# Seven edits in one kernel: sums through 2 KB rows, a merge order that lags one branch, chunked groups, quadrant matmuls, paired retention heads, norms moved behind other work, and a last tile in halves

## The chip, the cores and the metric

The kernel runs on one core of a Trainium2 chip. The metric is the device time of one execution, in microseconds (us); lower is better. Three executions of the kernel before took 3305.34 us in the median (3305.04 to 3309.78).

## The reference, cut to what matters

Two stacks of two layers each run over one sequence of 512 tokens with 1024 channels, all in float32.

```python
for l in range(2):                       # first_block
    h = rmsnorm(x, norm1_g[l]); p = h @ w_in[l]
    y_rw  = rwkv7_branch(...)            # 8 heads of 64, a state recurrence over 512 steps, group norm
    y_ret = retention_branch(...)        # 4 heads, scores * decay @ v, norm per head
    y_sg  = sgu_branch(...)              # 4 groups, spatial gating
    x = x + sum(sigmoid(gates) * (branch @ w_branch[l])) @ w_out[l]
    x = x + conv_ffn(rmsnorm(x, norm2_g[l]), ...)
x = rmsnorm(x, final_g)
for l in range(2):                       # second_block: five attention branches, same kind of merge
    x = _layer(x, mem, ...)
return rmsnorm(x, final_norm)
```

## The kernel before, in words

Activations lie channels by tokens: eight tiles of 128 channels x 512 tokens. Every weight is split into a rounded high part and a low rest (`whi`, `wlo`, by ScalarE at L159 and VectorE at L160), and every product is three matmuls (`mm3`, L168 to L170: high x high, high x low, low x high). A weight chunk is 128 x 1024 (512 KB); one chunk serves one output tile of 24 matmuls of 512 columns (`fm_tile`, `fm_steps`). Two chunks are in flight at most (two buffers each of raw, high and low).

In a layer of the first stack a planner (`Plan`) writes out the order of TensorE's instructions by hand. It knows dense steps (projections, cost 1.4 for six matmuls) and chain steps, which carry a cost and a wait after which the next step of that chain is due; dense steps fill the waits. Ranks: the projections of the rwkv branch first, then retention and gating unit (`branches`), then the 24 gate tiles (`gates1`). The chains are: `rw_pair` for each of four pairs of heads f, then `rwkv_inverse`, then two lanes of `rw_unit` (16 units per layer, each with the chain pst, psam, psv, psg, psh, psu, psy and psx), then `rw_final` per pair. A unit of pair f > 1 waits until `rw_final` of pair f - 2 has ended.

`sums` adds over the channels of a head: a matmul with a selector puts the sums of the four token groups on rows 32 g + i, a function makes the tile `sums` of them, a DMA writes this 128 x 128 tile to memory, and n DMAs (n is 2 for pairs, 1 for retention) read it back spread over all partitions, in pieces of 128 tokens (512 bytes). After a sum the chain waits 13 (L519), 10 (L737) or 11 (L750) units of the plan, and retention's `ret_end` 12.

`retention` takes one head after the other. Per head and token block j it makes scores with a contraction of 64 rows (`pssc`, L804; head e lies on rows 64 e to 64 e + 63), multiplies them with the decay (`pret`, L807), and accumulates `psret` (L809). `tm_group` projects token-major tiles: for each of four token groups it runs through both chunks of the contraction, 24 matmuls of 256 columns.

`merge` (after the plan; here the framework orders TensorE) goes through eight output tiles c and in each through the branches n, in the order retention, gating unit, rwkv. `pbr` is the branch product; each tile of the first stack holds 12 matmuls. Two PSUM banks serve `pm` and `pbr` in the first stack. `split` of the rwkv result is at L181 and L182.

`end_norm` and `end_norms` (between the stacks two norms in one) sum squares with tiny matmuls (`psn`), take root and reciprocal (`rcol`), and spread the result with matmuls (`psb`). At the start the splits of x, its squares and their sums are made tile by tile. At the end the last `w_out` tile is followed by `end_norm`, eight multiplications (L1816) and eight DMAs to the output.

Of the kernel before, what the change touches and what calls it, by code (L numbers as in the profile page):

```python
# [18 lines left out]
S = 512  # L19
D = 1024  # L20
# [86 lines left out]
class Kern:  # L107
# [7 lines left out]
    def __init__(self, tc, I, out, dbg=None, cfg=None):  # L115
        self.tc, self.nc, self.I, self.out = tc, tc.nc, I, out
        self.dbg_outs = dbg or {}
        self.cfg = cfg or {}
# [77 lines left out]
    def sums(self, x, sel, n, ps, out, fn):  # L196

        nc = self.nc
        for g in range(4):
            nc.tensor.matmul(ps[32 * g:32 * g + 32, :], lhsT=sel, rhs=x[:, g * 128:(g + 1) * 128],  # L200
                             start=True, stop=True, skip_group_check=True)
        t = self.ap.tile([128, 128], F32, name="sums", tag="sums", bufs=2)
        fn(t, ps)
        d = self.dp.tile([4, 32, 128], F32, name="sumd", tag="sumd", bufs=8)
        nc.sync.dma_start(d.rearrange("g r t -> (g r) t"), t)
        for i in range(n):
            nc.sync.dma_start(out[i * 128 // n:(i + 1) * 128 // n, :].rearrange("p (g t) -> p g t", g=4),
                              d[:, i][None].to_broadcast([128 // n, 4, 128]))
# [161 lines left out]
    def fm_steps(self, ws):  # L370

        ps = self.PM(name="pm")
# [6 lines left out]
    def tm_group(self, src, evac):  # L379

        ws = [self.weights(src[i], 1024) for i in range(2)]
        for g in range(4):
            ps = self.PM([128, 512])
            for k in range(KD):
                w = ws[k // 4]
                o = (k % 4) * 256
                hh = (self.h[k][0][:, g * 128:(g + 1) * 128], self.h[k][1][:, g * 128:(g + 1) * 128])
                self.mm3(ps[:, :256], hh, (w[0][:, o:o + 256], w[1][:, o:o + 256]), k == 0, k == KD - 1)
                if k == KD // 2 - 1:
                    yield MORE  # L390
            evac(g, ps[:, :256])
            yield MORE if g < 3 else TILE
# [73 lines left out]
    def rw_pair(self, l, f, r, k, vt, m, lora, half):  # L466
# [52 lines left out]
        yield Chain(0.4, 13.0)  # L519
# [89 lines left out]
    def rw_unit(self, f, g, st, lane):  # L609
# [79 lines left out]

        for c in range(2):  # L690
            psx = self.P([128, 2, 64], "psx")
            cs = slice(64 * c, 64 * c + 64)
            for e in range(2):
                os = ws = slice(64 - 64 * e, 128 - 64 * e)
                us = slice(64 * e, 64 * e + 64)
                b_ = tk[cs, 0, us]
                nc.tensor.matmul(psx[os, 0, :], lhsT=uw[cs, e, ws], rhs=b_, start=True, stop=True,
                                 skip_group_check=True)
                nc.tensor.matmul(psx[os, 1, :], lhsT=b_, rhs=uw[cs, e, us], start=True, stop=False,
                                 skip_group_check=True)  # L700
                nc.tensor.matmul(psx[os, 1, :], lhsT=tk[cs, 1, us], rhs=vp[cs, 3 * e, :], start=False, stop=True,
                                 skip_group_check=True)
            nc.vector.tensor_tensor(xt[:, 2 * g + c, :], psx[:, 0], self.ident64, op=OP.add)
            nc.scalar.activation(cc[:, 2 * g + c, :], psx[:, 1], AF.Copy)
        yield Chain(2.4, 0.5)

    def rw_final(self, l, f, st):
# [29 lines left out]
        yield Chain(0.4, 10.0)  # L737
# [12 lines left out]
        yield Chain(1.6, 11.0)  # L750
# [15 lines left out]
    def retention(self, l, win):  # L766
# [4 lines left out]
        for f in range(2):  # L771
# [18 lines left out]
            ws = self.stream([win[l, 22 + 2 * f], win[l, 23 + 2 * f]])  # L790
            for e in range(2):
                h = 2 * f + e
# [4 lines left out]
                dec = F(name="dec"); nc.sync.dma_start(dec, I["c_dec1"][h])  # L797
                yield Chain(0.0, 1.0)
                hs = slice(64 * e, 64 * e + 64)
                psy = self.PF(name="psret")  # L800
                for j in range(4):
                    n = S - 128 * j
                    ps = self.PF(name="pssc")
                    nc.tensor.matmul(ps[:, :n], lhsT=qk[1][hs, j * 128:(j + 1) * 128], rhs=qk[0][hs, j * 128:],  # L804
                                     start=True, stop=True)
                    p = T(name="pret")
                    nc.vector.tensor_tensor(p[:, :n], ps[:, :n], dec[:, :n], op=OP.mult)  # L807
                    yield Chain(0.3 + n / 1024, 3.2)
                    nc.tensor.matmul(psy[:, j * 128:], lhsT=vt[j // 2][:, j % 2, e * 128:(e + 1) * 128], rhs=p[:, :n],  # L809
                                     start=(j == 0), stop=(j == 3), skip_group_check=True)  # L810
                y = self.tile("Y", name="yret")
                sq = T(name="sqr")
                nc.scalar.activation(sq, psy, AF.Square)
                nc.vector.scalar_tensor_tensor(y, psy, 0.5, gt, op0=OP.mult, op1=OP.mult)
                yield Chain(0.4, 3.0)
                self.norms(sq, self.sel[:, 1], 1, self.PF([128, 128], "psrn"), bias=self.eps[:, 0:1], scale=1.0 / 128)
                self.plan.add(self.ret_end(l, h, y, sq), 0, 12.0)
                yield Dense(0.4)
# [104 lines left out]
    def merge(self, l, ys, wbr, wout, gain, stag=None, split=True):  # L923
        nc = self.nc
        nb = len(ys)
        s, late = [], []
        ws = self.stream(wbr[l])
        for c in range(KD):
            acc = None
            for n in range(nb):  # L930
                if (c, n) in self.gd:
                    g = self.F(name="gate")
                    nc.sync.dma_start(g, self.gd[c, n])
                else:
                    g = self.gate(self.gs, "F")
                nc.scalar.activation(g, g, AF.Tanh, scale=0.5)  # L936
                pb = self.fm_tile(ws, ys[n], name="pbr")
                with self.tc.high_priority(offset=self.cfg.get("hp", self.AHEAD)):
                    nc.vector.scalar_tensor_tensor(g, g, 1.0, pb, op0=OP.add, op1=OP.mult)  # L939
                if late and n == self.cfg.get("ln", 1):  # L940
                    s.append(self.split(late.pop(), *stag(c - 1), scale=0.5))
                if acc is not None:
                    (nc.gpsimd if self.pre and n in self.cfg.get("pa", (1, 2, 3)) else nc.vector).tensor_tensor(g, g, acc, op=OP.add)  # L943
                acc = g
            self.dump("%ss%d_%d" % (self.pre, l, c), acc)
            late.append(acc)
        s.append(self.split(late.pop(), *stag(c), scale=0.5))
# [3 lines left out]
        for c in range(KD):  # L951
# [8 lines left out]
            self.norm_step(c, x, gain(c) if gain else None, split=split)  # L960


    def ffn(self, l, next_gain, gain1, side):
# [32 lines left out]
        if gain1:  # L996
            self.end_norms()
        else:
# [204 lines left out]
    def block2_layer(self, l, gain):  # L1203
# [6 lines left out]
        self.zd = []  # L1210
        fill = self.gates(I["w_gt2"][l][10:], 5, self.cfg.get("e2", (5, 4, 4, 5, 4, 3, 4, 5)))
# [83 lines left out]
        self.end_norm(copy=gain is not None)  # L1295

    def col(self, name, scale=None, tag="F"):
        return self.evac2(self.fm_tile(self.ws), name, scale, tag)
# [461 lines left out]
    def run(self):  # L1760
# [3 lines left out]
        with ExitStack() as ctx:  # L1764
# [11 lines left out]
            if L1:  # L1776
                g12 = self.cp.tile([128, 8], F32, name="g12")
                nc.vector.tensor_tensor(g12, V[:, 16:24], V[:, 24:32], op=OP.mult)
                with block(self, "act"):
                    self.begin_norm()  # L1780
                    self.first = self.stream(I["w_in1"][0, 0:14])
# [309 lines left out]
```

## Time and profile before

| what | us |
|---|---|
| median of three executions | 3305.34 |
| the profiled execution | 3305.33 |
| its span in the profile | 3303.6 |
| TensorE busy (matmuls) | 3231.0 |
| VectorE busy | 2188.8 |
| ScalarE busy | 1365.9 |

The span is cut in windows and rows of time; a row of a timeline has its start, its length, the engine, the line, the operation, what is written and read, shapes and a count, and in brackets the idle time before it with what ended it. TensorE's matmuls are pipelined, so the length of a row overlaps the next; the time that a matmul takes is read from start to start. A matmul in plain float32 shows as two records. The granted clock 1.00 is 2.4 GHz, 0.50 is 1.2 GHz.

### The profile page before, as it was taken

The page shows a single profiled execution, that of the slowest core. Times are in us where ns is not written, and L with a number is a line of the kernel's source. Part 1 is how long each engine was busy: PE and PEld are TensorE (multiplying, and loading weights), DVE is VectorE, ACT ScalarE, POOL GpSimd, SP SyncE. Part 2 cuts the span into 40 slices and gives each one's busy share as a digit, 9 for nine tenths or more (in the row PEclk, how much of TensorE's full clock was granted, in tenths as well). Part 3 has the DMA queues.
Part 4 walks back from the last instruction along what each step waited for, and adds up shares of the span by engine and source line. Part 5 has one row for each costly group of instructions (what it writes and reads, how often), then busy time and mean ns, then how long its engine had stood idle before and what let it go on. Part 6 is the DMA issues. An engine that isn't in the chain of part 4 may idle for free.

```text
span 3303.6 us, 47422 instructions
## 1 busy us (share of the span) xinstructions
PE 3231.0 (98%) x17956; PEld 2594.5 (79%) x17960; DVE 2188.8 (66%) x4062; ACT 1365.9 (41%) x2440; POOL 125.6 (4%) x176
## 2 busy tenths in 40 slices
PE   8999999999999999999999999999999999999998
PEld 6787877888887787878888878877787888777777
DVE  6765656777537855646677446986666669866665
ACT  5433434444335333434444334344334443443443
POOL 0000000000000000000000000010003100100031
PEclk9999999999999999999999999999999999999999
DMA  4433245333433423246333437453455564533464
GB/s 146 124 94 96 74 136 170 128 107 96 137 112 105 130 75 91 80 139 189 102 99 99 150 108 212 134 159 104 121 185 197 172 170 138 152 113 121 152 209 140
DMA packets 198644, 434.75 MB, mean 132 GB/s; under 512 B 29704, under 2 KB 56456, under 8 KB 198416
## 3 DMA queue, kind: packets, MB, share of 16 engines
q1 hardware_dynamic: 197328, 429.62, 42.1%
q8 instruction: 142, 2.33, 0.3%
q0 software_dynamic: 512, 1.05, 0.1%
q10 hardware_dynamic: 576, 1.05, 0.1%
q14 instruction: 86, 0.70, 0.1%
HBM read 339.05 MB, written 61.36 MB: 121 GB/s over the span
## 4 chain that ended last, share of the span: by engine, by line
PE 84%; DVE 6%; DMA 6%; ACT 2%; issue 2%; SPq 1%; POOL 0%; DVEq 0%; ACTq 0%; POOLq 0%
PE pm L168 22%; PE pm L170 21%; PE pm L169 21%; PE psy L1152 2%; PE pbr L168 2%; PE pbr L169 2%; PE pbr L170 2%; PE pspt L1142 2%; DVE wlo L160 1%; PE psl L1124 1%; DMA sqr<-sumd 1%; PE psl L1125 1%; DMA rdw<-sumd 1%; ACT whi L159 1%; PE pssc L804 1%
## 5 line engine op out<-in xcount | busy, mean ns | idle before, releaser
L168 PE MATMUL pm<-shi,whi 128*128 128x512 f32 x3072 | 1231.7, 401 | 8.8 <-ACT whi L159 7.9
L170 PE MATMUL pm<-shi,wlo 128*128 128x512 f32 x3072 | 1207.4, 393 | 1.1 <-DVE wlo L160 1.0
L169 PE MATMUL pm<-slo,whi 128*128 128x512 f32 x3072 | 1206.1, 393 | 1.8 <-DVE slo L185 1.8
L159 ACT ACTIVATE whi<-wraw 128x1024 fp32r<-128x1024 f32 x480 | 509.3, 1061 | 884.4 <-PE pm L169 533.3
L160 DVE TENSOR_TENSOR wlo<-wraw,whi 128x1024 fp32r<-128x1024 f32 x480 | 588.1, 1225 | 206.1 <-ACT whi L159 199.6
L168 PEld LDWEIGHTS pm<-shi,whi 128*128 128x128 f32 x3072 | 578.6, 188 | 147.4 <-issue 26.8
L170 PEld LDWEIGHTS pm<-shi,wlo 128*128 128x128 f32 x3072 | 578.1, 188 | 127.6 <-DVE wlo L160 4.8
L169 PEld LDWEIGHTS pm<-slo,whi 128*128 128x128 f32 x3072 | 578.7, 188 | 117.2 <-DVE slo L185 4.4
L424 DVE TENSOR_TENSOR ev<-pm,rb 128x512 f32<-128x512 f32 x140 | 96.1, 686 | 113.6 <-PE pm L170 113.1
L894 DVE TENSOR_TENSOR gate<-pm,rb 128x512 f32<-128x512 f32 x80 | 55.1, 688 | 128.5 <-PE pm L170 128.4
L168 PE MATMUL pbr<-shi,whi 128*128 128x512 f32 x288 | 115.0, 399 | 14.0 <-ACT shl L181 10.4
L168 PE MATMUL pm<-whi,shi 128*128 128x256 f32 x384 | 115.0, 300 | 7.1 <-ACT whi L159 7.1
L169 PE MATMUL pm<-wlo,shi 128*128 128x256 f32 x384 | 111.7, 291 | 3.7 <-DVE wlo L160 3.6
L170 PE MATMUL pbr<-shi,wlo 128*128 128x512 f32 x288 | 113.1, 393 | 0.0
L169 PE MATMUL pbr<-slo,whi 128*128 128x512 f32 x288 | 113.1, 393 | 0.0
L170 PE MATMUL pm<-whi,slo 128*128 128x256 f32 x384 | 111.1, 289 | 0.0
L939 DVE SCALAR_TENSOR_TENSOR gate<-gate,pbr 128x512 f32<-128x512 f32 x128 | 85.8, 683 | 31.8 <-PE pbr L170 31.1
L943 POOL TENSOR_TENSOR gate<-gate 128x512 f32<-128x512 f32 x48 | 78.3, 1630 | 593.1 <-DVE gate L939 337.0
L936 ACT ACTIVATE gate<-gate 128x512 f32<-128x512 f32 x128 | 75.9, 626 | 42.2 <-DMA gate<-gtd 39.9
L1109 ACT ACTIVATE p<-psl,st 128x256 f32<-128x256 f32 (+3 forms) x128 | 65.2, 513 | 61.0 <-DVE st L1107 51.6
L168 PEld LDWEIGHTS pm<-whi,shi 128*128 128x128 f32 x384 | 76.0, 198 | 9.8 <-ACT whi L159 7.7
L169 PEld LDWEIGHTS pm<-wlo,shi 128*128 128x128 f32 x384 | 76.3, 199 | 4.7 <-DVE wlo L160 4.5
(506 smaller groups left out, 4465.8 us busy)
## 6 DMA issues: line engine op xcount, KB each, us to landing
wraw<-in_w_gt SPq DMA_DIRECT2D x148, 512.0 KB, 3.7
wraw<-in_w_in SPq DMA_DIRECT2D x116, 512.0 KB, 3.7
wraw<-in_f_up SPq DMA_DIRECT2D x88, 512.0 KB, 3.5
gtd<-gate SPq DMA_DIRECT2D x116, 256.0 KB, 2.0
gate<-gtd SPq DMA_DIRECT2D x116, 256.0 KB, 4.0
wraw<-in_w_br SPq DMA_DIRECT2D x44, 512.0 KB, 3.7
wraw<-in_f_dn SPq DMA_DIRECT2D x44, 512.0 KB, 3.5
wraw<-in_w_out SPq DMA_DIRECT2D x32, 512.0 KB, 3.7
```

The lines of the kernel that those rows point to most:

```text
L159: nc.scalar.activation(hi[:, :n], raw[:, :n], AF.Copy)
L160: nc.vector.tensor_tensor(lo[:, :n], raw[:, :n], hi[:, :n].bitcast(F32), op=OP.subtract)
L168: nc.tensor.matmul(ps, lhsT=lhs[0], rhs=rhs[0], start=first, stop=False, skip_group_check=skip)
L169: nc.tensor.matmul(ps, lhsT=lhs[0], rhs=rhs[1], start=False, stop=False, skip_group_check=skip)
L170: nc.tensor.matmul(ps, lhsT=lhs[1], rhs=rhs[0], start=False, stop=last, skip_group_check=skip)
L424: self.last = self.nc.vector.tensor_tensor(t, ps, self.rb, op=OP.mult)
L936: nc.scalar.activation(g, g, AF.Tanh, scale=0.5)
L939: nc.vector.scalar_tensor_tensor(g, g, 1.0, pb, op0=OP.add, op1=OP.mult)
L943: (nc.gpsimd if self.pre and n in self.cfg.get("pa", (1, 2, 3)) else nc.vector).tensor_tensor(g, g, acc, op=OP.add)
L1109: nc.scalar.activation(p[:, :w], l, AF.Exp, bias=st[:, 0:1], accum_out=st[:, 1:2])
L1142: nc.tensor.transpose(pt_[:, b * 128:(b + 1) * 128], ps[e][:, b * 128:(b + 1) * 128], self.ident)
L1152: nc.tensor.matmul(psy[64 * e:64 * e + 64, :], lhsT=vs[e][b], rhs=pts[e][:, b * 128:(b + 1) * 128], start=first and b == 0, stop=last and ...
```

## The change

- `sums`: the tile goes to memory as n DMAs of four rows (rows i, i + 32, i + 64, i + 96), into a tensor [n, 4, 128], and each of the n reads takes one row of 512 tokens (2 KB) to its partitions. The waits after it go from 13 to 10, 10 to 7.5, 11 to 8.5, and 12 to 10 + e.
- `tm_group`: two PSUM banks hold the four token groups; the loop over the two weight chunks is outside. Each chunk is asked for when its turn comes.
- psx in `rw_unit`: the same 12 matmuls of 64 x 64, ordered so that four following ones go to the four quadrants of the array; both PSUM tiles are taken first.
- `retention`: both heads' gates first, then both heads' scores next to each other per token block j (on PSUM tag `pw` instead of `pf`), then both heads' products. The decay tiles move to tag Y. 12 chain stops per pair of heads become 6.
- `merge` of the first stack: branch 2 (rwkv) of tile c comes after branches 0 and 1 of tile c + 1; the weights are laid out in that order.
- Between the stacks: the first two projections of the second stack (`early`) are put ahead of `end_norms`.
- Start: all eight splits first, then squares and sums; the first two projection tiles use the two PF banks. End: the last `w_out` tile in two halves of 256 tokens, each with its own norm, multiplications and output DMAs (`finish`).

```diff
@@ sums
-        d = self.dp.tile([4, 32, 128], F32, name="sumd", tag="sumd", bufs=8)
-        nc.sync.dma_start(d.rearrange("g r t -> (g r) t"), t)
+        d = self.dp.tile([n, 4, 128], F32, name="sumd", tag="sumd%d" % n, bufs=8)
         for i in range(n):
-            nc.sync.dma_start(out[i * 128 // n:(i + 1) * 128 // n, :].rearrange("p (g t) -> p g t", g=4),
-                              d[:, i][None].to_broadcast([128 // n, 4, 128]))
+            nc.sync.dma_start(d[i], t[i:128:32, :])
+        for i in range(n):
+            nc.sync.dma_start(out[i * 128 // n:(i + 1) * 128 // n, :],
+                              d[i].rearrange("g t -> (g t)")[None].to_broadcast([128 // n, S]))
@@ tm_group
-        ws = [self.weights(src[i], 1024) for i in range(2)]
-        for g in range(4):
-            ps = self.PM([128, 512])
-            for k in range(KD):
...
+        ps = [self.PM([128, 2, 256]) for _ in range(2)]
+        for i in range(2):
+            w = self.weights(src[i], 1024)
+            for g in range(4):
+                for k in range(4):
...
+                    self.mm3(ps[g // 2][:, g % 2], hh, ww, i == 0 and k == 0 and g % 2 == 0, i == 1 and k == 3, skip=True)
+                if i and g % 2:
+                    evac(g - 1, ps[g // 2][:, 0])
+                    evac(g, ps[g // 2][:, 1])
@@ rw_unit
+        psx = [self.P([128, 2, 64], "psx") for _ in range(2)]
+        for m in range(3):
+            for e in range(2):
+                for c in range(2):
...
+                    nc.tensor.matmul(psx[c][os, o, :], lhsT=x, rhs=y, start=first, stop=last, skip_group_check=True)
@@ retention
+            psy = [self.PF(name="psret") for _ in range(2)]
+            for j in range(4):
+                n = S - 128 * j
+                ps = [self.P(name="pssc") for _ in range(2)]
+                for e in range(2):
+                    hs = slice(64 * e, 64 * e + 64)
+                    nc.tensor.matmul(ps[e][:, :n], lhsT=qk[1][hs, j * 128:(j + 1) * 128], rhs=qk[0][hs, j * 128:],
                                      start=True, stop=True)
+                p = [T(name="pret") for _ in range(2)]
+                for e in range(2):
+                    nc.vector.tensor_tensor(p[e][:, :n], ps[e][:, :n], decs[e][:, :n], op=OP.mult)
+                yield Chain(0.4 + n / 600, 3.6)
...
@@ merge
-        for c in range(KD):
-            acc = None
-            for n in range(nb):
+        for c, n in merge_order(nb):
...
+        if not split:
+            self.finish(wo, s)
@@ block2_layer
+        if l == 0 and self.sq2 is not None:
+            self.early = [self.fm_tile(self.ws) for _ in range(2)]
+            self.end_norms()
@@ run
-                        self.norm_step(c, self.x_get(c), vg(0)(c), eng=nc.gpsimd if c in self.cfg.get("pe", ()) else None)
+                        xs.append(self.x_get(c))
+                        self.h.append(self.split(xs[c], tag="h", scale=vg(0)(c)))
...
+                    for x in xs:
+                        self.sq = self.add_square(self.sq, x)
+                    self.banks = [self.PF(), self.PF()]
@@ merge_order
+    if nb != 3:
+        return [(c, n) for c in range(8) for n in range(nb)]
+    o = []
+    for c in range(9):
+        o += [(c, 0), (c, 1)] * (c < 8) + [(c - 1, 2)] * (c > 0)
+    return o
```

The new function `finish`, cut:

```python
for hf in range(2):
    cs = slice(256 * hf, 256 * hf + 256)
    ps = self.PM()
    for k in range(KD):
        self.mm3(ps[:, 0:256], ww[k], [t[:, cs] for t in s[k]], k == 0, k == KD - 1)
    nc.vector.tensor_tensor(x[:, cs], ps[:, 0:256], x[:, cs], op=OP.add)
    ...                                  # square, psn, rcol, psb for this half
    for c, t in enumerate(self.xlast):
        nc.vector.scalar_tensor_tensor(t[:, cs], t[:, cs], self.vlast(c), ps[:, 0:256], op0=OP.mult, op1=OP.mult)
        (nc.sync if c % 2 else nc.scalar).dma_start(self.out[c][:, cs], t[:, cs])
```

## Rows read from the trace of the kernel before

**Rows 1.** The page, busy time of each engine.

```profile
PE 3231.0 (98%) x17956; PEld 2594.5 (79%) x17960; DVE 2188.8 (66%) x4062; ACT 1365.9 (41%) x2440; POOL 125.6 (4%) x176
```

**Rows 2.** TensorE's waits: who waited for whom, us, times, longest.

```profile
PE pm L168 <- ACT whi L159: 15.0, 4, 7.9
PE pbr L168 <- ACT shl L181: 10.4, 2, 5.4
...
PE psA L542 <- DVE kkr L529: 2.9, 3, 1.5
PE psb L192 <- DVE rcol L340: 2.4, 1, 2.4
```

**Rows 3.** Windows, TensorE alone: length, busy (records), granted clock, DMA share, GB/s.

```profile
8.00:22.00 14.00, 12.16 (x45) 1.00 0.86 287
118.00:129.40 11.40, 6.07 (x28) 0.70 0.61 174
509.60:518.50 8.90, 3.84 (x10) 0.62 0.20 76
1082.90:1091.90 9.00, 4.80 (x21) 0.62 0.49 133
...
1942.20:1956.50 14.30, 7.34 (x33) 0.64 0.44 139
3287.80:3303.60 15.80, 3.94 (x17) 0.57 0.36 133
```

**Rows 4.** Timeline of ScalarE and TensorE at the start.

```profile
15.99 0.62 ACT L299 ACTIVATE sq<-x 128x512 f32<-128x512 f32 x1
...
18.66 0.50 PE L169 MATMUL pm<-slo,whi 128*128 128x512 f32 x1 [0.30 <-DVE slo L185]
```

**Rows 5.** Timeline of TensorE around one chain step (psw, psa).

```profile
46.51 0.39 PE L169 MATMUL pm<-slo,whi 128*128 128x512 f32 x1
46.73 0.39 PE L170 MATMUL pm<-shi,wlo 128*128 128x512 f32 x1
47.05 0.69 PE L473 MATMUL psw<-mix,lora 64*128 64x512 f32 x1
47.06 0.69 PE L475 MATMUL psa<-mix,lora 64*128 64x512 f32 x1
...
48.11 0.50 PE L168 MATMUL pm<-shi,whi 128*128 128x512 f32 x1
48.45 0.39 PE L169 MATMUL pm<-slo,whi 128*128 128x512 f32 x1
```

**Rows 6.** Timeline of TensorE around one head's first scores.

```profile
145.10 1.12 PE L804 MATMUL pssc<-ev 64*128 64x512 f32 x2
146.16 0.50 PE L168 MATMUL pm<-shi,whi 128*128 128x512 f32 x1
```

**Rows 7.** Timeline of TensorE around one unit's psx.

```profile
211.12 0.33 PE L697 MATMUL psx<-tk,uw 64*64 64x64 f32 x2
...
212.12 0.50 PE L168 MATMUL pm<-shi,whi 128*128 128x512 f32 x1
```

**Rows 8.** Timeline of TensorE in a token-major group of layer 1.

```profile
1082.58 0.28 PE L169 MATMUL pm<-wlo,shi 128*128 128x256 f32 x1
1082.70 0.28 PE L170 MATMUL pm<-whi,slo 128*128 128x256 f32 x1
```

**Rows 9.** Timeline of VectorE at the first merge.

```profile
511.19 0.69 DVE L752 TENSOR_TENSOR y<-y,rdw 128x512 f32<-128x512 f32 x1 [3.76 <-DMA rdw<-sumd]
```

**Rows 10.** DMA issues: queue, count, KB each, median us from issue to landing.

```profile
sqk<-sumd SPq DMA_DIRECT2D x32, 128.0 KB, 5.8
...
sqr<-sumd SPq DMA_DIRECT2D x8, 256.0 KB, 8.5
...
cumb<-cumd SPq DMA_DIRECT2D x8, 256.0 KB, 3.7
```

**Rows 11.** Timeline of VectorE at the end.

```profile
3294.66 5.36 DVE L1816 SCALAR_TENSOR_TENSOR x<-x,vecg,psb 128x512 f32<-128x512 f32 x8 [2.23 <-PE psb L317]
```

## The prediction made before the run

> **What bounds the kernel now.** I read the page first: TensorE is busy 3231.0 of 3303.6 us, VectorE 2188.8, and nothing else comes near [rows 1]. So time goes only where TensorE has fewer matmuls, waits less, or waits less at the half clock. Second, who TensorE waited for: 15.0 us in four waits on a weight's high part, 10.4 in two on the rwkv split at the merges, small ones on the norms [rows 2]. Third, windows around these waits; they show that a wait costs more than itself, for the granted clock falls in it and the matmuls behind it run partly at 1.2 GHz [rows 3]. Fourth, the timeline from start to start, for the price of each kind of matmul. The profiled execution took 3305.33 us, its span and 1.7 around it, and the median is 3305.34, so span and result can be added to and taken from alike.
>
> Prices: a 512-column matmul follows the one before after 0.22 to 0.23 us [rows 5]; a 256-column one after 0.12 [rows 8]. A stop of a chain costs TensorE 0.32 before it in place of 0.22, and 0.34 behind it, so some 0.2 us on top of its own matmuls [rows 5].
>
> **The change part by part.**
>
> *Token-major groups.* In both layers the first of these groups ran 12 matmuls on the first chunk and then waited for the second. The windows hold 11.4 us with 28 records and 9.0 with 21, at granted clocks 0.70 and 0.62 [rows 3]. At 0.12 each the records are worth 3.4 and 2.5, so 8.0 and 6.5, together 14.5 us, are lost. In the new order the first chunk feeds 48 matmuls, 5.8 us in place of 1.4, which covers all but some 1 us of each wait; the second chunk's load is asked for in the same place on SP, behind the same swaps. I take 12; bounds 7 (the load comes later) to 14.5. ScalarE evacuates two groups at once, at half and at the end; the third group's bank was taken at the start, so no matmul waits for it.
>
> *Merges of the first stack.* The first window is 8.9 us with 10 records, worth 2.3 at 0.227: 6.6 lost [rows 3]; the second layer waits as long (10.4 in two waits, the longest 5.4) [rows 2], so 13.2 in all. What is late is the last pair's final: VectorE sat 3.76 us for the spread rows of its last sum [rows 9]. Two more tiles of 12 matmuls, 5.4 us, now stand ahead of the first that needs the rwkv result. Also that sum's rows come sooner and the chain's waits are shorter, so gates are left to fill. Next late would be the gate tiles' loads, which SP issues ahead already. I take 13; bounds 8 and 13.2.
>
> *Sums.* Forty sums. The read of 256 KB in pieces of 512 bytes takes 8.5 us, that in rows of 2 KB 3.7 (`cumb`); the reads of a pair, two of 128 KB, take 5.8 at psk [rows 10]. So the read is 2.5 to 4.8 us shorter, and the waits written in the plan are 3, 2.5, 2.5 and 1 to 2 shorter: the data come about as much earlier as TensorE asks for them. The visible waits there are 2.9 us in three [rows 2]; I leave them. SP issues one DMA more for a pair, plain ones; weight loads queued behind them move by well under a microsecond. Gain 0; bounds -6 to +3. The gain of the shorter chain is in the merges, counted above.
>
> The Trainium skill, page "DMA: Bandwidth & Descriptors", section "Rules for kernel authors", says that a DMA whose outermost dimension is under 16 runs on at most that many engines, and so the new writes of four rows on four. No row here shows such a write of sums; the rule would change the rival of the late sums below and not the sum.
>
> *psx by quadrants.* One unit's 24 records take 1.00 us from the first to the next projection [rows 7], of which about 0.15 is the switch. The old order sends six records to one quadrant, then six to the next, and the records overlap by two at a time. If four run at once, half of 0.85 goes. I take 0.35 a unit; 32 units give 11; bounds 0 (no more than two at once) and 14.
>
> The Trainium skill, page "TensorE: Matmul & The Clock Gate", section "Wait — 56ns, not 53.3ns?", says that starts never follow closer than about 25 ns. By it 24 records would take 0.6 us at least, and this part would give 8 (an estimate from that page). The trace has starts 10 ns apart, psw at 47.05 and psa at 47.06 [rows 5], so I don't go by it.
>
> *Scores of two heads.* psw and psa, two products of 64 rows on different halves of the array, take 1.06 us together (47.05 to 48.11) [rows 5], as much as one pssc of the same size alone (145.10 to 146.16) [rows 6]. Put next to each other, two heads' scores should cost as one. A head has 1280 columns, 2.5 times 1.06 or 2.65 us; four pairs save 10.6. Bounds 0 and 11.7. Besides, 6 stops less per pair of heads, 24 in all at 0.2: 4.8. Against it: pssc moves to the four banks that the lanes use too, and a chain step now waits for two VectorE products; I take 2 off, so 2.8, bounds -4 to 4.8.
>
> *Between the stacks.* The window from the last FFN tile to the first projection is 14.3 us with only tiny matmuls, 7.34 us of them at a granted clock of 0.64 [rows 3]. At the full clock they would take about 3.7 (half, an estimate). The two early projections, 11 us of matmuls, need the split tiles and weights that are there, and cover the last squares and the table load. What stays is 3.7 and the wait for root and reciprocal, 2.4 [rows 2]. So 14.3 - 3.7 - 2.4 = 8.2; bounds 5 and 10.6. Their two banks of three stay taken until `rb` comes; the next product that needs one finds the third.
>
> *Start.* The window 8 to 22 us holds 45 records [rows 3], 29 of them projections (6.6 us) and 16 tiny ones (some 1.8): 5.6 lost. The last matmuls of the first tile wait for the splits (18.66), between which ScalarE made eight squares of 0.62 [rows 4]. Without these the last split is done some 4 us sooner, a good part of which is projections; the norm then comes about when it did, and two more banks hold what is ready. I take 3.4; bounds 1 and 5.
>
> *End.* Now 15.8 us follow the last matmul [rows 3], with eight multiplications of 5.36 [rows 11]. The halves cost 48 x 0.12 against 24 x 0.227, +0.4, and the first half's norm matmuls on top, some 1.5. Behind the last matmul the multiplications are half as wide (2.7 to 5.4; I take 3.3), add, square and norm are shorter too, and the clock may still be up. Net 2.5; bounds -2 (ScalarE's queue holds output DMAs that wait for the first half's multiplications, ahead of the second half's square) and 5.
>
> Sum: 12 + 13 + 0 + 11 + 10.6 + 2.8 + 8.2 + 3.4 + 2.5 = 63.5 us. 3305.3 - 63.5 = 3241.8.
>
> **The rivals.**
>
> *The matmuls don't run side by side.* Then psx and the scores give nothing: 63.5 - 21.6 = 41.9, or 3263 us. For it: nowhere do four 64 x 64 products overlap. Against it: psw and psa [rows 5].
>
> *The waits move.* With less work on TensorE the chain of the lanes stays the length it has, the gates run out sooner, and half of groups, merges and stacks (33 us) comes back as new waits: 3258 us. For it: the gates ended just as the last sum was due. Against it: the chain gets shorter, by some 3 units for f = 3 and 5 at each final that a later pair waits for.
>
> *Sums come later than the plan asks: slower.* Per layer eight waits that TensorE sees (four psk, four psmean) were cut by 3 and 2.5. If the new reads are no faster and the writes slower, each stops TensorE, and the half clock behind it doubles the price. From 63.5 / 16 = 4.0 us a stop the change loses; at 5 us it ends at 3322. Against it: 8.5 against 3.7 [rows 10].
>
> *More comes back.* All upper bounds but two hold: some 18 us more, 3224.
>
> **How the numbers follow.** Forecast 3242 with chance 0.62; not side by side 0.12; waits move 0.12; more comes back 0.08; slower 0.04; the rest, 0.02, within 0.2%, about what a measurement of this kernel can tell from no change. The range takes in both smaller gains and the upper bounds: 3219 to 3268. Faster 0.94, same 0.02, slower 0.04.
>
> **What would show it.** In the changed kernel: no wait of over 2 us of the groups on `wlo`/`whi` and none at the merges on the rwkv split; the window between the stacks filled with projections, granted clock 1.00; psx from first to next projection 0.6 to 0.7 us; two pssc starts some 10 ns apart; `sumd` reads at 3 to 4 us. I am wrong if psA or psq wait several us each on `kkr` or the squares, or if the lanes' alternation shows new gaps.

## The result, and the profile after

The changed kernel takes 3269.48 us (median of 4 runs, 3266.67 to 3272.18) against 3305.19 for the kernel before on the same chip: a ratio of 0.9891, 95% interval 0.9874 to 0.9908. That is 35.7 us less, where 63.5 were forecast. The time lies 1.5 us above the upper end of the range. The profiled execution has a span of 3268.5 us.

The stages tell where the 28 us are missing. The table is worked out from the first records of `psw`, `pbr`, `psn` and `psl` in the two TensorE timelines; "13.0 kept" is the first experiment below, shown here because it answers the table.

| stage, us | before | after | forecast of the difference | difference | 13.0 kept |
|---|---|---|---|---|---|
| start, to the first `psw` | 47.1 | 45.7 | -3.4 | -1.4 | 45.5 |
| plan of layer 0, `psw` to the first merge tile | 451.7 | 445.2 | | -6.5 | 432.2 |
| plan of layer 1 | 453.9 | 449.9 | | -4.0 | 432.2 |
| both plans (groups, sums, psx, scores, visits) | 905.6 | 895.1 | -36.4 | -10.5 | 864.4 |
| merges and output of both layers | 240.6 | 225.1 | -13 | -15.5 | 225.1 |
| second FFN and what stands between the stacks, norm ahead of it to the first `psl` | 431.3 | 425.7 | -8.2 | -5.6 | 425.9 |
| last norm but one of the second stack to the end | 676.5 | 673.9 | -2.5 | -2.6 | 671.9 |

So most of the missing time is in the two plans, which gave 10 us in place of 36; the start and the stretch between the stacks gave 2.0 and 2.6 less than forecast. In the plans the new matmuls do what was said. TensorE's timeline around one pair of scores and around one unit's psx, in the changed kernel (start and duration in us, engine, line, operation, output and inputs, shape, count):

```profile
149.41 1.13 PE L812 MATMUL pssc<-ev 64*128 64x512 f32 x4
150.47 0.50 PE L170 MATMUL pm<-shi,whi 128*128 128x512 f32 x1
...
206.62 0.34 PE L706 MATMUL psx<-tk,uw 64*64 64x64 f32 x8
206.79 0.30 PE L706 MATMUL psx<-uw,tk 64*64 64x64 f32 x8
206.91 0.30 PE L706 MATMUL psx<-vp,tk 64*64 64x64 f32 x8
207.13 0.39 PE L170 MATMUL pm<-whi,shi 128*128 128x256 f32 x1
```

The 24 records of psx take 0.51 us to the next projection, half of [rows 7], and four records of two heads' scores take 1.06, as two of one head did [rows 6]. The Trainium skill, page "TensorE: Matmul & The Clock Gate", section "Wait — 56ns, not 53.3ns?", with its some 25 ns between starts, would make psx 0.6 us at least (an estimate from that page); the trace has 0.51 with the switch in it, so products on four quarters of the array start closer together than that section says, and the measurement decides.

Who TensorE waited for in the changed kernel (us in all, times, longest):

```profile
PE psA L548 <- DVE kkr L535: 14.3, 5, 5.2
PE pf L170 <- ACT whi L161: 7.1, 1, 7.1
PE psz L724 <- DVE cc L718: 5.8, 2, 2.9
PE psam L653 <- ACT rhs L637: 4.8, 3, 1.8
PE psY L734 <- ACT cc L709: 3.8, 4, 1.6
...
PE psam L653 <- DVE y L736: 2.8, 2, 1.4
PE psz L724 <- DVE am L658: 2.7, 2, 1.4
```

The groups' waits on a weight's split and the merges' on the rwkv split [rows 2] are gone; the 7.1 us on `whi` that stay are the first weight of the run, where the kernel before waited 7.9. psA, the product at the end of a pair's chain, waited 2.9 us there and now 14.3; this is one of the forecast's signs of being wrong. psam (the lanes) and psz and psY (a pair's final), which were small, come up beside it. In the two plans the gaps between TensorE's records sum to 37.0 us, against 19.3 in the kernel before. TensorE by windows in the changed kernel (length, busy and records, granted clock, DMA share, GB/s):

```profile
93.00:100.00 7.00, 6.12 (x49) 0.51 0.21 75
121.00:130.00 9.00, 9.00 (x72) 1.00 0.34 93
490.90:603.50 112.60, 112.60 (x498) 1.00 0.56 172
1926.80:1943.00 16.20, 13.26 (x90) 1.00 0.33 98
3252.00:3268.50 16.50, 7.81 (x60) 0.76 0.38 127
```

The group (121 to 130), the merges (490.9 to 603.5) and the stretch between the stacks (1926.8 to 1943) run at the full clock, where [rows 3] had 0.70, 0.62 and 0.64. The first window is the new loss: behind the longest wait for psA the granted clock is 0.51, the lower of the two levels, for nearly 7 us.

### The profile page after: what moved, and what is told of

Same layout as the page of the kernel before. It is cut to its first block, busy times and chain, and to the rows that moved or that the text cites. A ratio compares the mean times of both kernels' runs of the same rounds, so it can differ in the third digit from the quotient of the medians.

```text
span 3268.5 us, 47563 instructions
## 1 busy us (share of the span) xinstructions
PE 3195.0 (98%) x17992; PEld 2575.6 (79%) x17992; DVE 2189.7 (67%) x4071; ACT 1356.9 (42%) x2438; POOL 123.9 (4%) x176
## 4 chain that ended last, share of the span: by engine, by line
PE 84%; DVE 8%; DMA 3%; ACT 2%; issue 2%; SPq 0%; POOL 0%; DVEq 0%; ACTq 0%; POOLq 0%
PE pm L170 22%; PE pm L172 21%; PE pm L171 21%; PE pbr L170 2%; PE pbr L171 2%; PE pbr L172 2%; PE psy L1197 2%; DVE wlo L162 2%; PE pspt L1187 2%; PE psl L1169 1%; ACT whi L161 1%; PE psl L1170 1%; DMA sqk<-sumd 1%; DMA gate<-gtd 1%; DVE R L586 1%
```

## Why psA waits

In `rw_pair` the squared keys of a pair are summed (`psk`), ScalarE takes the root and VectorE the reciprocal, `sums` writes the result to memory and reads it back spread, VectorE makes `kkr` of it in several steps, and `psA` is the product of `kkr` and `kr`. This is the second pair's chain in the changed kernel. `psk` runs at 71.18, and at 88.69 TensorE has no other work left in front of psA. ScalarE:

```profile
70.91 3.24 ACT L554 ACTIVATE CP<-psA 32x128 f32<-32x128 f32 x8
...
75.45 1.28 ACT L494 ACT_TABLE_LOAD   x1
76.74 0.31 ACT L494 ACTIVATE sums<-sums 128x128 f32<-128x128 f32 x1
```

VectorE, to the last factor of psA (in brackets: idle before it, and what ended that):

```profile
79.32 0.94 DVE L495 RECIPROCAL sums<-sums 128x128 f32<-128x128 f32 x1
...
87.27 0.75 DVE L529 SCALAR_TENSOR_TENSOR kkr<-mix,vec,sqk 128x512 f32<-128x512 f32 x1 [3.41 <-DMA sqk<-sumd]
...
89.60 0.69 DVE L534 SCALAR_TENSOR_TENSOR kkr<-a,kkr 128x512 f32<-128x512 f32 x1
90.20 1.22 DVE L499 TENSOR_TENSOR_SCAN sc<-c_reset,sw 128x512 f32<-128x512 bf16 x1
91.33 0.67 DVE L430 TENSOR_TENSOR ev<-pm,rb 128x512 f32<-128x512 f32 x1
91.92 1.22 DVE L162 TENSOR_TENSOR wlo<-wraw,whi 128x1024 fp32r<-128x1024 f32 x1
93.05 0.69 DVE L535 SCALAR_TENSOR_TENSOR kkr<-kkr,sc 128x512 f32<-128x512 f32 x1
```

And TensorE:

```profile
93.88 1.61 PE L548 MATMUL psA<-kr,kkr 64*64 64x64 f32 x32 [5.19 <-DVE kkr L535]
95.42 0.79 PE L170 MATMUL pm<-shi,whi 128*128 128x512 f32 x1
96.01 0.63 PE L171 MATMUL pm<-slo,whi 128*128 128x512 f32 x1
```

From psk to psA are 22.7 us; in the kernel before the second pair took 23.2 (71.22 to 94.39). The read did get shorter, though not by the 3 us that were taken off the wait: SP issues it 12.1 us behind psk, and its rows are there 4.0 later, where they took 5.3 in the kernel before (78.83 to 84.13). But the reciprocal, and with it the write, comes 3.1 us later than before (79.32 against 76.22), for the shorter wait has put the first pair's eight evacuations of psA, 3.24 us, and a table load ahead of the root on ScalarE. The first experiment, with the old wait behind psk, shows the other order on ScalarE:

```profile
71.10 0.31 ACT L494 ACTIVATE sums<-sums 128x128 f32<-128x128 f32 x1 [1.28 <-DVE sums L493]
...
74.64 3.32 ACT L554 ACTIVATE CP<-psA 32x128 f32<-32x128 f32 x8
```

There the reciprocal starts 4.2 us behind psk (69.71, 73.90); in the changed kernel it is 8.1, in the kernel before 5.0. So VectorE gets to `kkr` at 87.27 in the changed kernel; in the kernel before it was 87.75, and there it did not wait for rows. Behind it VectorE makes another pair's scan, an evacuation and a weight split (3.1 us, in the kernel before the same three) before psA's last factor. The product `psbon`, whose step in the plan stands behind the shortened wait, came 4.8 us sooner (82.68 against 87.46); psA's last factor came 0.6 us sooner (93.05 against 93.66).

## The experiments

All are the changed kernel with the edit shown. Times are medians of four runs; the kernel before took 3301.9 to 3306.4 beside them. Five of these kernels, whose edits turned out to pay nothing against each other, take 3235 to 3237 on four chips, so I take some 2 us as the accuracy of a difference; where one of the five ran on the same chip as an edit, the difference taken from it is within 1 us of the one given.

**The sums taken apart.** The wait behind psk put back, in `rw_pair`:

```diff
-        yield Chain(0.4, 10.0)
+        yield Chain(0.4, 13.0)
```

> The changed kernel with one number put back: the wait behind the key sums psk is 13.0 in the plan again, not 10.0 (eight places, four a layer); everything else as changed. Theory A, the wait was cut further than the chain got shorter: from psk to the ready psA the changed kernel takes 22.7 us for the second pair where the kernel before took 23.2, so TensorE asks 5 us too early. Put back, psA waits under 3 us in all (14.3 now), the half-clock windows at 93 and 1042 us go, and the time falls by 12 to 20 us, to about 3253. Theory B, the waits move: the lanes are bound by VectorE and ScalarE, not by where TensorE stands, so 10 us of new waits come up at the lanes, the finals or the merges, and the time stays within 5 us of 3269.

Measured: 3235.98 us, ratio 0.9800 (0.9785 to 0.9815); 33.5 us faster than the changed kernel, 17 faster than theory A had, and 6 faster than the forecast for the whole change (3241.8). Theory A's side, with more than it gave. The gaps in both plans sum to 14.9 us in place of 37.0. Its TensorE waits:

```profile
PE psam L653 <- ACT rhs L637: 5.8, 4, 1.6
...
PE psz L724 <- DVE cc L726: 1.8, 4, 0.8
...
PE psA L548 <- DVE kkr L535: 1.1, 4, 0.3
```

psA is hardly asked for too early any more (1.1 us in all), and the stops at psz and psY went too, which I had not expected.

All four waits put back:

```diff
-        yield Chain(0.4, 10.0)
+        yield Chain(0.4, 13.0)
...
-        yield Chain(0.4, 7.5)
+        yield Chain(0.4, 10.0)
...
-        yield Chain(1.6, 8.5)
+        yield Chain(1.6, 11.0)
...
-                self.plan.add(self.ret_end(l, 2 * f + e, ys[e], sqs[e]), 0, 10.0 + e)
+                self.plan.add(self.ret_end(l, 2 * f + e, ys[e], sqs[e]), 0, 12.0)
```

> The changed kernel with all four waits put back (13.0 behind psk, 10.0 behind psmean, 11.0 behind psq, 12.0 for the end of a retention head), rows of 2 KB kept. Theory A, only the wait behind psk was cut too far, since nothing waits on the other sums: within 4 us of the run with 13.0 alone, about 3253, and the finals end 7 us later per layer, which the merges' two extra tiles (5.4 us) cover only in part, so perhaps 2 to 6 us slower than that run. Theory B, the waits move: 3265 to 3275, with waits on the rwkv split at the merges again.

Measured: 3244.92, ratio 0.9824 (0.9808 to 0.9840). Between the theories: still 24.6 faster than the changed kernel, but 8.9 slower than with 13.0 alone, and not at the merges, where no wait came back: the plans are 5.1 and 4.3 us longer, with a stop of 3.5 and one of 3.0 us at psam behind psz.

The old `sums` (one write, reads in pieces of 512 bytes) with the shorter waits, and with all four old waits:

```diff
-        d = self.dp.tile([n, 4, 128], F32, name="sumd", tag="sumd%d" % n, bufs=8)
-        for i in range(n):
-            nc.sync.dma_start(d[i], t[i:128:32, :])
+        d = self.dp.tile([4, 32, 128], F32, name="sumd", tag="sumd", bufs=8)
+        nc.sync.dma_start(d.rearrange("g r t -> (g r) t"), t)
...
```

> The changed kernel with the sums' rows of 512 bytes as before (one write, two reads of four pieces), and the shorter waits kept. Theory A, the reads are on the path of every sum that TensorE waits for: the read took 5.8 us at psk before, and the spread rows came 4.9 us later behind the second psk (16.5 less 7.6 us, against 4.0 now), so psA waits some 3 to 5 us more at each of eight places and psq some more: slower than the changed kernel by 20 to 45 us, 3290 to 3315. Theory B, VectorE's and ScalarE's queues set when the sums come out, and the rows are hidden behind them: within 5 us of 3269.

> The changed kernel with the old rows of 512 bytes and all four old waits: the sums' part of the change undone as a whole. Theory A: the waits of TensorE on the sums are then those of the kernel before (psA 2.9 us), and the rest of the change keeps its gain, so this is 10 to 18 us faster than the changed kernel, some 3255, and within 6 us of the run with new rows and old waits. Theory B, the rows of 2 KB carry the gain at the merges: the last pair's sums come late again, waits on the rwkv split of 5 us a layer come back, and it is 3270 to 3280.

Measured: 3328.38, ratio 1.0079 (1.0064 to 1.0094), and 3272.37, ratio 0.9910 (0.9895 to 0.9925). With the short waits the old rows cost 59 us, more than theory A had; with the old waits they cost 27.5 (3272.4 against 3244.9), and there the time is theory B's, but its reason is missing: psA waits only 5.0 us, and the merges are 112.6 us long as in the changed kernel. The price is in the plans again (449.5 and 448.7 us), and VectorE's waits show it, here in the kernel with old rows and old waits:

```profile
DVE yret L834 <- DMA sqr<-sumd: 29.2, 7, 6.6
...
DVE y L742 <- DMA cc<-sumd: 8.8, 6, 2.5
DVE kkr L527 <- DMA sqk<-sumd: 8.8, 5, 3.6
...
DVE y L755 <- DMA rdw<-sumd: 5.3, 2, 2.7
```

and in the one with new rows and old waits:

```profile
DVE y L744 <- DMA cc<-sumd: 4.3, 2, 2.6
DVE y L757 <- DMA rdw<-sumd: 3.0, 2, 2.0
```

52.1 against 7.3 us, and 1.2 in one wait for a retention head that the view of `sumd` lists: 8.5. An instruction that waits at the head of VectorE's queue for the rows of a retention head holds up the lanes' masks behind it. One place with the old rows, VectorE:

```profile
286.66 0.69 DVE L834 TENSOR_TENSOR yret<-yret,sqr 128x512 f32<-128x512 f32 x1 [5.36 <-DMA sqr<-sumd]
287.37 1.75 DVE L656 TENSOR_TENSOR am<-psam,c_rwmask 64x256 f32<-64x256 f32 x4
```

and TensorE:

```profile
288.37 0.41 PE L660 MATMUL psv<-vp,am 128*128 128x64 f32 x2 [2.17 <-DVE am L656]
```

So the rows of 2 KB pay less where TensorE waits for a sum itself (psA 5.0 us with the old rows, 1.1 with the new) than where VectorE does. The edit changes the write, the read and the number of buffers of `sumd` together; no run takes these apart.

**How early is too early.** 11.5 and 14.5 behind psk:

> The changed kernel with 11.5 behind psk, half way between 10.0 (3269 us) and 13.0 (3236). Theory A, the price grows with how much too early psA is asked for: the chain from psk to psA is 17.6 to 22.7 us long, by what else stands in VectorE's and ScalarE's queues, so at 11.5 the longest still stop TensorE by some 2 to 3 us each: 3244 to 3256. Theory B, 10.0 is a point at which the pairs' steps fall on top of each other (the eight evacuations of one psA, 3.24 us, ahead of the next pair's root), and just above it there is nothing to lose: 3234 to 3240.

> The changed kernel with 14.5 behind psk, longer than before the change. Theory A, the price lies in asking too early alone: from 13.0 on nothing is lost at psA, each pair's chain is 1.5 us longer in the plan and gates fill it, so 3233 to 3240. Theory B, the plan is greedy and each value gives another arrangement of lanes and finals, better or worse by up to 10 us a layer: anything from 3230 to 3256, with no stop at psA but others at psam, psz or psY.

Measured: 3256.07, ratio 0.9854 (0.9839 to 0.9869), and 3236.80, ratio 0.9789 (0.9772 to 0.9805). So 10.0, 11.5, 13.0 and 14.5 give 3269, 3256, 3236 and 3237: it falls, and is flat from 13.0 on, as theory A of both has it, but not for A's reason: at 11.5 psA has no wait of its own left, so only some 13 of the 33.5 us go with its stops. The other 20 go with stops at psz, psY and psam, which are about the same at 10.0 and 11.5.

The last three steps to psA put ahead in VectorE's queue, at 10.0:

```diff
+        with self.tc.high_priority(offset=self.AHEAD):
             nc.vector.tensor_tensor(kr[:, :, 0, :], g4(kkr), g4(e0), op=OP.mult)
             nc.vector.scalar_tensor_tensor(bd, a, 1.0, kkr, op0=OP.add, op1=OP.mult)
             nc.vector.scalar_tensor_tensor(bd, bd, 0.5, ei, op0=OP.mult, op1=OP.mult)
```

> The changed kernel, 10.0 behind psk as changed, but the last three VectorE steps ahead of psA stand further ahead in VectorE's queue: of the 6.4 us from the first to the last step of the second pair, another pair's scan of 1.22, an evacuation of 0.67 and a weight split of 1.22 are taken out from between. Theory A, the queue makes up part of the chain: psA's long waits (5.2 and 4.7) fall to some 2 each, psA in all to 6 to 8 us, and the time by 8 to 14, to 3256 to 3262. Theory B, the rows of the sums come too late whatever follows: within 4 us of 3269.

Measured: 3263.19, ratio 0.9874 (0.9857 to 0.9890). psA's waits fall from 14.3 to 8.2 us (longest 3.0) and the time by 6.3: the queue is part of the chain, as theory A said, though the time gained is less than the 8 I gave as its least.

**What the other 20 us are.** At 11.5, TensorE and VectorE around the third pair's final. VectorE:

```profile
364.70 0.41 DVE L658 TENSOR_TENSOR am<-psam,c_rwmask 64x256 f32<-64x256 f32 x1
365.03 0.67 DVE L882 TENSOR_TENSOR ysg<-ysg,ev 128x512 f32<-128x512 f32 x1
365.71 3.04 DVE L658 TENSOR_TENSOR am<-psam,c_rwmask 64x256 f32<-64x256 f32 x7
368.77 0.62 DVE L718 TENSOR_TENSOR cc<-cc,ds 128x448 f32<-128x448 f32 x1
```

TensorE:

```profile
369.54 0.33 PE L724 MATMUL psz<-cc,xt 64*64 64x64 f32 x4 [2.92 <-DVE cc L718]
```

Both lanes ask for psam at once, so VectorE has eight masks to make in a row, and the scaling of `cc`, from which the final starts, stands behind them. With 13.0 the lanes stand some 2 us apart there, and the scaling goes ahead of the masks. The experiment puts it ahead, at 11.5:

```diff
+        with self.tc.high_priority(offset=self.AHEAD):
             nc.vector.tensor_tensor(cc[:, 0:7, :], cc[:, 0:7, :], d[:, 0:7].unsqueeze(2).to_broadcast([128, 7, 64]), op=OP.mult)
```

> The changed kernel with 11.5 behind psk (3256 us) and the scaling of cc, the first step of a pair's final, ahead of the lanes' copies and masks in VectorE's queue. Theory A, the arrangement costs through this queue: the stop of 2.9 us at psz in each layer goes, with up to 3.4 us of half clock behind it, 6 to 9 us in all, 3247 to 3250. Theory B, the stop only moves to the lanes' psam or psv, whose masks are now later: 3253 to 3259.

Measured: 3248.47, ratio 0.9828 (0.9813 to 0.9843), 7.6 less: theory A. VectorE scales at 362.56, ahead of the masks, and TensorE finds it:

```profile
369.09 0.33 PE L725 MATMUL psz<-cc,xt 64*64 64x64 f32 x4
```

The other 12 us, the stops at psam and psY, were not tried one by one, and their cause stays open; that they too are meetings of lanes and finals on VectorE and ScalarE is argued from their releasers alone.

**The other waits, at 13.0 behind psk.** The retention's 12.0, then the finals' 10.0 and 11.0:

> The changed kernel with 13.0 behind psk and the old wait of 12.0 before the end of a retention head (10.0 and 11.0 as changed). Theory A, retention's ends are off the path of the lanes: within 3 us of 3236. Theory B, the second group's ends meet the finals on VectorE, and the stop of 3.5 us at psam behind psz that all four old waits showed comes back: 3240 to 3246.

> The changed kernel with 13.0 behind psk and the finals' old waits, 10.0 behind psmean and 11.0 behind psq. Theory A, the finals' waits are the ones that pay, since the lanes' next pair starts only when the final two before it has ended: 5 us less in each final, so 3241 to 3247. Theory B, within 3 us of 3236.

Measured: 3235.36, ratio 0.9787 (0.9772 to 0.9801), nothing; and 3247.66, ratio 0.9822 (0.9807 to 0.9837), 11.7 slower, more than theory A had. The lanes may start a pair only when the final two before it has ended, so a shorter final is worth time to all behind it. Its largest new wait:

```profile
PE psam L653 <- DVE cc L726: 6.0, 2, 3.3
```

**The other parts, each undone at 13.0 behind psk.** The groups, psx and the retention as they were (for each its part of the diff above, in reverse), and the old order of the merges, in `merge_order`:

```diff
-    if nb != 3:
+    if True:
```

> The changed kernel with the wait of 13.0 behind psk (3236 us) and, beside that, the token-major groups as before: four banks one after the other, each over both chunks. Theory A, with the sums in time TensorE is the bound again (15 us idle in both plans together), and each part is worth what its records say: the stalls of 8.0 and 6.5 us on the second chunk come back, 12 to 15 us, so 3248 to 3251. Theory B, the lanes set the plan's end: half of that or less, under 3243.

> The changed kernel with 13.0 behind psk and, beside that, psx as before: one chunk after the other, six records to a quadrant. Theory A: 32 units at 1.00 in place of 0.50 us, 16 us of TensorE, so 3250 to 3253. Theory B, a lane's chain sets the end and TensorE has room beside it: under 3243. The forecast's own step took 0.35 a unit, 11 us, 3247.

> The changed kernel with 13.0 behind psk and, beside that, the merges of the first stack in the old order, the rwkv branch third of each three tiles and not two tiles later. Theory A, the order is what took the 13 us of waits away: 3247 to 3250, with waits of some 5 us a layer on the rwkv split. Theory B, the shorter sums alone bring the last final forward enough: the waits stay away and the time within 4 us of 3236. Each layer's final ends some 7 us sooner by the shorter waits behind psmean and psq, so I expect the truth between, 3 to 8 us slower.

> The changed kernel with 13.0 behind psk and, beside that, retention head by head on the three banks of before. Theory A: scores and visits are worth their records, pssc 10 to 11 and psret and the stops 4 to 5 us, so 3249 to 3252. Theory B, the pairs cost as much elsewhere (they take the lanes' banks, and their norms' reciprocals stand ahead of the first lanes' copies, where psam waits 1.6 and 1.3 us): 3236 to 3243, with the first psam waits gone.

Measured: groups 3249.51 (0.9834, 0.9820 to 0.9849), 13.5 slower, theory A, with `pm <- whi` waiting 6.2 us; psx 3245.74 (0.9824, 0.9810 to 0.9839), 9.8 slower, between the theories: the records cost 8 us more in each plan, the plan is 4.2 longer; order of the merges 3235.11 (0.9793, 0.9779 to 0.9808), nothing, and no wait on the rwkv split, theory B; retention 3252.83 (0.9846, 0.9830 to 0.9862), 16.9 slower, a little more than theory A had.

The lanes 2.5 us later, and the old order between the stacks:

```diff
-            yield Chain(0.0, 26.0)
+            yield Chain(0.0, 28.5)
...
-        if not gain1:
+        if gain1:
+            self.end_norms()
+        else:
             self.end_norm()
...
-            self.early = [self.fm_tile(self.ws) for _ in range(2)]
-            self.end_norms()
+            pass
```

> The changed kernel with 13.0 behind psk and the lanes' start 2.5 us later in the plan (28.5 behind the start of the inverse in place of 26.0). Theory A, the first two psam (waits of 1.6 and 1.3 us in each layer, 6.8 us at half clock behind them) are asked for ahead of VectorE's last step of the inverse, so the stop and the half clock go: 6 us a layer, 3224 to 3230. Theory B, the lanes set when the plan ends: what is won at their start is lost at their end, 3234 to 3240.

> The changed kernel with 13.0 behind psk and, between the stacks, the order of before: the norms first, then the first two projections of the second stack. Theory A, the forecast's step holds: 8 us slower, 3243 to 3246. Theory B, what the stages show: the stretch from the last norm of the first stack to the first scores of the second is 5.5 us shorter in the changed kernel, so 3240 to 3243. Theory C, the two projections only move: within 2 us of 3236.

Measured: 3236.60 (0.9792, 0.9778 to 0.9807), nothing: the first psam wait 0.8 and 1.0 us at most in place of 1.6, and later stops take their place (psz 5.5 us in place of 1.8), theory B. And 3243.39 (0.9814, 0.9799 to 0.9828), 7.4 slower, at the edge between theories A and B.

## Why the prediction was wrong, and where it was right

**Sums: the step that failed.** The forecast put the part at nothing, with 6 us of loss at most, because the reads became 2.5 to 4.8 us shorter and the waits 3, and "the data come about as much earlier as TensorE asks for them". It was not one term near zero but four, of which three are large: rows of 2 KB at the old waits +27.5; the finals' shorter waits +11.7; the retention's 0; the shorter wait behind psk -33.5. (The finals' and the retention's put back together cost 8.9, not 11.7, so the terms depend on each other; taken one behind the other they give 27.5 + 8.9 - 33.5 = 2.9.) That the net, 2.9 us, lies inside the bounds of the term is luck and no support for the step. The read is one leg of four between psk and psA; the others (root and reciprocal, the write, three factors) stand in the queues of ScalarE and VectorE, and got later as the pairs moved together. The row that should have warned is in [rows 2]: psA already waited 2.9 us in three places with 13.0, so there was no slack of which to take 3, and [rows 10] gave the read alone. The bound of -6 came from no row at all, while the forecast's own rival of the late sums reckoned with stops of 4 and 5 us.

**The other sentence on the sums** that failed is that their shorter chain pays in the merges. It pays in the plans, on VectorE. In [rows 9] VectorE sat 3.76 us for rows of a sum; I read it as one late final, and not as a kind of wait that stands in front of the lanes. VectorE's waits in the kernel before have 52.2 us of it:

```profile
DVE y L752 <- DMA rdw<-sumd: 18.5, 6, 4.1
...
DVE yret L822 <- DMA sqr<-sumd: 12.0, 2, 6.6
DVE kkr L523 <- DMA sqk<-sumd: 11.1, 5, 4.7
DVE y L739 <- DMA cc<-sumd: 10.6, 4, 4.0
```

**The adding up** failed with it. With the sums as before, rows and waits, the other parts, 63.5 us in the forecast, give some 30 (3272.4 against 3301.9 beside it), and the two plans 7.4 of their 36.4. VectorE's waits for rows are there as before (52.1 us), and the gaps between TensorE's records in the plans are 36.1 us in place of 19.3. So what the parts save in TensorE's records comes back there as gaps; with the rows of 2 KB and 13.0 behind psk the plans are 41.2 us shorter. The forecast added the parts as if TensorE alone set the length of a plan. That the waits for rows are what takes the gain back is read from these runs; it was not followed step by step.

**Merges: the gain right, the cause half.** 15.5 us against 13. The new order takes the waits away with the old sums (112.6 us there), and the shorter sums take them away with the old order (112.6 too): either is enough, so with both the order is worth nothing.

**Groups, psx, scores, between: right, once the sums are in time.** Undone one by one at 13.0 behind psk: 13.5 (forecast 12), 9.8 (11), 16.9 (10.6 and 2.8), 7.4 (8.2). psx is right by two errors: the records gave 16 us, not 11, and some 6 of these did not reach the time.

**Start: too high.** 1.4 against 3.4. ScalarE still makes a square between every two splits; the changed kernel's rows:

```profile
14.10 0.71 ACT L186 ACTIVATE shi<-x,vecg 128x512 fp32r<-128x512 f32 x1
14.71 0.62 ACT L303 ACTIVATE sq<-x 128x512 f32<-128x512 f32 x1
15.23 0.71 ACT L186 ACTIVATE shi<-x,vecg 128x512 fp32r<-128x512 f32 x1
```

The squares were written behind the splits in the program, and I took the program's order for the queue's. And of the 5.6 us that I counted as lost, some 2 are the first nine matmuls, which follow each other after 0.4 to 0.7 us in both kernels, where later ones take 0.23. **End:** 2.6 against 2.5, and the multiplications behind the last matmul take 3.22 us, where I took 3.3.

**The rivals.** Products side by side: settled by the rows above. Late sums: its mechanism is what happened, at psk and not at psmean, at 4 of 8 places for more than 1.5 us; its sign did not come, for it priced all sixteen. The time of the first, 3263, came nearest to 3269.5, though its mechanism is refuted: luck. The waits move, 3258: saved work did come back as waits in the plans, but the lanes were not the limit it said they were, since one number put back gives 3236. Writes of four rows, by the Trainium skill's "DMA: Bandwidth & Descriptors", section "Rules for kernel authors", spread over at most four engines: for the second pair SP issues the read 3.0 us behind the write (80.29, 83.27), where it was 1.6 in the kernel before (77.19, 78.83). Over the sixteen sums of psk the median is 2.7 against 2.3, but with the old waits 2.5 with the new writes against 2.9 with the old. So no run here shows that rule clearly as a loss, and none excludes a small one.

## What to carry to other kernels

A wait written into a plan is not the length of its DMA: it covers a chain through the queues of several engines, here a root, a reciprocal, a write, a read and the factors behind it. The read got 1.3 us shorter at the second pair, the wait 3.0, and the chain 0.5. Asked for too late, psk costs nothing here (13.0 and 14.5 are the same), but the finals, which the lanes wait for, cost 11.7 us with 2.5 more behind each sum. Asked for too early, a sum costs its stop, the lower clock behind it and the order of what follows; at 11.5 psk cost 20 us with no stop at psA. The right value was found here by trying four. And a faster DMA is to be looked for at the engine whose queue stands still for its result: there it freed 44 us of VectorE's waits, and 27 of the kernel's time.

## What was not expected of the hardware

Four 64 x 64 products on four quarters of the array, eight records, start within 0.17 us (206.62 to 206.79) and the next eight records within 0.12, some 15 to 21 ns each. The forecast had taken 0.6 to 0.7 us for the whole of psx; the trace has 0.51.
